# The first modulations of a two-block transformer kernel: four column-tiled products on TensorE in place of VectorE sums

## The chip, the cores and the metric

One core of a Trainium2 chip. The metric is the device time of one execution in microseconds (us); the kernel before is given as the median of three runs. TensorE (PE) does matrix products, with its weight loads shown apart as PEld; VectorE (DVE) and ScalarE (ACT) do the elementwise work; SyncE (SP) issues nearly all loads from memory, in the order of its queue.

## The reference, cut to what matters

Two transformer blocks run one after the other over 256 tokens of 1024 numbers, all in f32. The first block begins with a modulation: a vector `c` (for the tokens) and a vector `c_ctx` (for 256 context tokens) each go through silu and are multiplied by the matrix `w_ada`, 1024 rows by 6144 columns. Only the first 2048 columns, the shift and the scale ahead of attention, are touched here:

```
mod_x = silu(c) @ w_ada + b_ada        # sh1 = columns 0..1023, sc1 = columns 1024..2047, ...
mod_c = silu(c_ctx) @ w_ada + b_ada
h  = rms_norm(x, g_attn) * (1 + sc1) + sh1
hc = rms_norm(ctx, g_attn) * (1 + csc1) + csh1
```

`h` and `hc` then go through the q, k and v projections, attention, a mixture of 32 experts (12 MB of weights each), and a second block with its own modulations.

## The kernel before

Everything named here is in `attention_block`. An order of the instructions on each engine is worked out by a planner when the program is built, from its own estimate of the times; each engine then keeps that order and waits where an input is late. An instruction later in the program text can be put ahead of an earlier one that is not expected to be ready. `high_priority` raises the rank of what stands under it, and the modulation steps for later use (`ada_step`) run at a lowered rank (LOW1).

Start. SP loads x and ctx (L317, L319) and then, through the stream `g.w1`, the eight 1 MB tiles that hold the 2048 columns. They go into a pool of four buffers (NSTAGE), so that tile 4 can be loaded only when one of the first four has been used up. The same pool and the same queue serve the projections' weights (`in_w_qkv`), which come right behind. `cs` is silu of the two vectors, 128 partitions by 2 by 8. PE normalizes and transposes x and ctx (L349) and transposes x once more (L354); ACT copies the results out (L350, L355).

Modulations. ADA1 gives the order in which the eight tiles come: four of them hold 1024 shift columns for 256 rows, the other four 512 scale columns for 512 rows. `shifts` multiplies a tile by the vector's numbers, one partition at a time, and adds it to `acc`, on DVE (L368, L370), sixteen operations on 128x1024. `scales` does the rest as products on PE with two stationary columns (L379), copies the rows out on ACT (L383) and turns them into columns (L386). At the end sixteen products with ones (L394) sum `acc` over the partitions. The results stand in `pt`; DVE makes `mod` of them in three small operations (L397, L399, L400).

What `mod` starts. ACT makes `hh` (L418, sixteen operations), DVE the rest `hl` (L420, L422), and PE the first projection from them (L593). The projection's weights are split beforehand in halves of a tile: ACT makes `hi` (L141), DVE `lo` (L142); three halves are made ahead of the first use. DVE also sums the later modulations from half-tiles of `w_ada` and `ada_w` (L190, L192), one operation for each 0.5 MB load, with two buffers of their own.

The experts' products further on (L918) show one form that matters here: `products` sends two products with 64 stationary columns each to the two halves of one bank of PSUM,

```
on = o[n] if e == WIDE else o[0][n * SLOTS:(n + 1) * SLOTS]
g.got = pe.matmul(out=on, lhsT=x, rhs=w[:, n * 512:n * 512 + 512], start=first, stop=last)
```

Of the kernel before, what the change touches and what calls it, by code (L numbers as in the profile page):

```python
# [8 lines left out]
F32 = mybir.dt.float32  # L9
# [4 lines left out]
ALU = mybir.AluOpType  # L14
# [7 lines left out]
NL0 = 8  # L22
ADA_PLACES = 30
LOW1 = 200

ADA1 = (0, 1, 0, 1, 0, 0, 1, 1)
ADA1_SUM = 7
ADA_RET = 12
ADA_F0 = 12
ADA_D0 = 4  # L30
# [25 lines left out]
def bc(ap, dim, n):  # L56

    a = list(ap.ap)
    a.insert(dim, [0, n])
    return bass.AP(tensor=ap.tensor, offset=ap.offset, ap=a)  # L60
# [89 lines left out]
def rsqrt(nc, pool, ss, n, scale, tag, e=None):  # L150

    v, e = nc.vector, e or nc.vector
    x = ss if scale is None else pool.tile([128, n], F32, tag=tag + "x", name="rsx")
    y, h, t = (pool.tile([128, n], F32, tag=tag + k, name="rs" + k) for k in "yht")
    if scale is not None:
        v.tensor_scalar(out=x, in0=ss, scalar1=scale, scalar2=EPS, op0=ALU.mult, op1=ALU.add)
    v.tensor_scalar(out=y.bitcast(I32), in0=x.bitcast(I32), scalar1=-0.5, scalar2=float(0x5F3759DF), op0=ALU.mult, op1=ALU.add)
    e.tensor_scalar(out=h, in0=x, scalar1=-0.5, scalar2=None, op0=ALU.mult)
    for _ in range(3):
        if n <= 2:  # L160
            cols = [slice(i, i + 1) for i in range(n)]
            for i in cols:
                e.tensor_scalar(out=t[:, i], in0=y[:, i], scalar1=y[:, i], scalar2=h[:, i], op0=ALU.mult, op1=ALU.mult)
            for i in cols:
                e.tensor_scalar(out=y[:, i], in0=t[:, i], scalar1=1.5, scalar2=y[:, i], op0=ALU.add, op1=ALU.mult)
        else:
            v.tensor_tensor(out=t, in0=y, in1=y, op=ALU.mult)
            v.tensor_tensor(out=t, in0=t, in1=h, op=ALU.mult)
            v.scalar_tensor_tensor(out=y, in0=t, scalar=1.5, in1=y, op0=ALU.add, op1=ALU.mult)
    return y  # L170
# [123 lines left out]
def attention_block(tc, g):  # L294

    nc, A, ws = tc.nc, g.A, g.ws
    v, s, pe = nc.vector, nc.scalar, nc.tensor
    xT1 = g.xT1
    with ExitStack() as es:
# [6 lines left out]
        def bank(name="b"):  # L306
            return ps.tile([128, 512], F32, tag="b", name=name)

        def bank1(tag):
            return pss.tile([128, 512], F32, tag=tag, name=tag)  # L310
# [3 lines left out]
        pl = es_x.enter_context(tc.tile_pool(name="pl", bufs=1))  # L314
# [13 lines left out]
        cs = c1.tile([128, 2, 8], F32, name="cs")  # L328
# [26 lines left out]
            s.copy(out=xT1[:, k:k + 2], in_=b.rearrange("p (k t) -> p k t", k=2))  # L355


        pt = bank("pt")
        acc = [pl.tile([128, 1024], F32, name=f"acc{j}") for j in range(2)]

        def shifts(i):
            w = g.w1.get()
            for k in range(2):
                wk = w[:, k * 1024:(k + 1) * 1024]
                for j in range(2):
                    cc = cs[:, j, 2 * i + k:2 * i + k + 1]
                    if i == k == 0:
                        v.tensor_scalar(out=acc[j], in0=wk, scalar1=cc, scalar2=None, op0=ALU.mult)  # L368
                    else:
                        v.scalar_tensor_tensor(out=acc[j], in0=wk, scalar=cc, in1=acc[j], op0=ALU.mult, op1=ALU.add)  # L370

        def scales(i):
            w = g.w1.get()
            b4, h = divmod(i, 2)
            if h == 0:
                pms.append(bank("pm"))
            pm = pms[-1]
            for k in range(4):
                pe.matmul(out=pm[:2, :], lhsT=cs[:, :, h * 4 + k], rhs=w[:, k * 512:(k + 1) * 512],  # L379
                          start=(h == 0 and k == 0), stop=(h == 1 and k == 3))  # L380
            if h == 1:
                row = pl.tile([2, 512], F32, tag="row", name="row")
                s.copy(out=row, in_=pm[:2, :])  # L383
                for j in range(4):
                    m = 8 + b4 * 4 + j
                    pe.transpose(out=pt[:, 2 * m:2 * m + 2], in_=row[:, j * 128:(j + 1) * 128], identity=g.ident[:2, :2])  # L386

        pms = []
        for i, kind in enumerate(ADA1):
            (scales if kind else shifts)(sum(k == kind for k in ADA1[:i]))  # L390
            if i == ADA1_SUM:
                for j in range(2):
                    for m in range(8):
                        pe.matmul(out=pt[:, 2 * m + j:2 * m + j + 1], lhsT=acc[j][:, m * 128:(m + 1) * 128], rhs=g.ones[:, :1], start=True, stop=True)  # L394
        mod = c1.tile([128, 16, 2], F32, name="mod")
        with tc.high_priority():
            v.tensor_tensor(out=mod, in0=pt[:, :32].rearrange("p (m j) -> p m j", j=2),  # L397
                            in1=bc(g.pv("b_ada")[:, :16], 2, 2), op=ALU.add)
            v.tensor_scalar(out=mod[:, 8:], in0=mod[:, 8:], scalar1=1.0, scalar2=None, op0=ALU.add)  # L399
            v.tensor_tensor(out=mod[:, 8:], in0=mod[:, 8:], in1=bc(g.pv("g_attn"), 2, 2), op=ALU.mult)  # L400

# [13 lines left out]
        for k in range(8):  # L415
            for j in range(2):
# [4 lines left out]
                                scalar2=mod[:, k, j:j + 1], op0=ALU.mult, op1=ALU.add)  # L421
# [181 lines left out]
        for t in range(4):  # L603
# [7 lines left out]
            else:  # L611
                v.tensor_tensor(out=ko[:, kt].rearrange("p (n d) -> p n d", d=64), in0=kq.rearrange("p (n d) -> p n d", d=64),
                                in1=bc(gn[:, 2], 1, 2), op=ALU.mult)
        r = rsqrt(nc, sm, sk, 8, 1.0 / 64, "k")
        v.tensor_tensor(out=ko.rearrange("p t (n d) -> p (t n) d", d=64), in0=ko.rearrange("p t (n d) -> p (t n) d", d=64),
                        in1=bc(r, 2, 64), op=ALU.mult)
# [11 lines left out]
        r = rsqrt(nc, sm, sq, 16, 1.0 / 64, "q")  # L628
        for t in range(2):
            q2 = tp.tile([128, 512], F32, tag="qq", name="qq")  # L630
            v.tensor_tensor(out=q2.rearrange("p (c j d) -> p j c d", j=2, d=64),
                            in0=qo[t].rearrange("p (j c d) -> p j c d", j=2, d=64),
                            in1=bc(r[:, 8 * t:8 * t + 8], 2, 64).rearrange("p (j c) d -> p j c d", j=2), op=ALU.mult)
# [17 lines left out]
        for t in range(2):  # L651
# [8 lines left out]
            for m in range(2):  # L660
                r = slice(64 * m, 64 * m + 64)
# [16 lines left out]
        shifts = o1.tile([128, 1024], F32, name="shifts")  # L678
# [11 lines left out]
        acc = bank1("t")  # L690
# [1207 lines left out]
def tile_body(ctx, tc, A, out):  # L1898
# [85 lines left out]
    g.s5dram = [nc.dram_tensor(f"s5_scratch_{c}", (128, S5W), F32, kind="Internal").ap() for c in range(8)]  # L1984
    g.s5E = [nc.dram_tensor(f"s5_scratch_e{c}", (128, 2, 16, 64), F32, kind="Internal").ap() for c in range(2)]
    attention_block(tc, g)
    g.ws.stream.load(19, es_hx.enter_context(tc.tile_pool(name="hx", bufs=1, side="right")).tile([128, 2048], F32, name="hx"))
    g.angp = ctx.enter_context(tc.tile_pool(name="angp", bufs=1))
# [13 lines left out]
def host_arrays(inputs):  # L2002
    import numpy as np

    def cat(*a):
        return np.ascontiguousarray(np.concatenate(a, axis=0))

    def colblocks(w, nb, kper):

        K, N = w.shape  # L2010
        t = w.reshape(K // (128 * kper), kper, 128, N // nb, nb).transpose(3, 0, 2, 1, 4)
        return t.reshape(-1, 128, kper * nb)
# [5 lines left out]
    d = {}  # L2018
    d["x"], d["ctx"] = I["x"][0], I["ctx"][0]
    wa = I["w_ada"][0]  # L2020
    ada1 = cat(colblocks(wa[:, :1024], 1024, 2), colblocks(wa[:, 1024:2048], 512, 4))
    d["w_ada1"] = ada1[np.argsort(np.argsort(ADA1, kind="stable"))]
    d["w_ada2"] = colblocks(wa[:, 2048:], 1024, 2)
    wq = I["w_qkv"][0]
    d["w_qkv"] = cat(colblocks(wq[:, 512:768], 256, 8), colblocks(wq[:, :512], 512, 4),
# [26 lines left out]
    cs = [I[f"s5_{n}_2"][0].reshape(8, 4, 2, 16, 64).transpose(0, 2, 4, 1, 3).reshape(8, 128, 4, 16) for n in ("c_re", "c_im")]  # L2052
# [20 lines left out]
    f = np.float32  # L2073
# [5 lines left out]
    row = np.broadcast_to(np.arange(4, dtype=f)[:, None], (4, 64)).reshape(-1)  # L2079
# [3 lines left out]
    c, s = np.cos(ang).astype(f), np.sin(ang).astype(f)  # L2083
# [28 lines left out]
```

## Time and profile before

| | |
|---|---|
| median of 3 runs | 2090.07 us (2088.04 to 2090.89) |
| the profiled execution | 2090.91 us |
| its span, first to last instruction | 2089.2 us |
| TensorE clock, mean over the span | 0.977 of full speed |
| busy: PE, DVE, ACT | 93%, 54%, 31% of the span |
| read from memory | 626.79 MB, 307 GB/s over the span |

The profile is of one execution. The busy share of PE counts time in which a product is under way, and does not mean that PE works at its peak. All times in the rows count from the first instruction of the span. In a row of the timeline the first two numbers are start and duration, then come the engine, the line, the operation and the tiles (written <- read), the shape and the count; in brackets is the idle time of the engine ahead of it and what ended that.

### The profile page before, as it was taken

Reading aid. Unit: us, or ns where it says so; the run is one execution under the profiler, and the core shown is the slowest. Engines: PE = TensorE matmul, PEld = TensorE weight load, DVE = VectorE, ACT = ScalarE, POOL = GpSimd, SP = SyncE. Lnnn points to the kernel's source line nnn. Section 1 sums busy time; section 2 is a strip of 40 time slices with the busy share of each in tenths; the row PEclk is TensorE's granted clock in tenths of the full one; section 3 lists DMA queues with packets and bytes.
Section 4 is the critical chain, followed back from the end, with each engine's and each line's share of the span. In section 5 each row is a group of like instructions: output and inputs, shape, how many; then the busy total and the mean of one; then the engine's idle time right before and its main releaser. Section 6 shows DMA issues by size and latency. Waiting matters only on the chain. (4 is left out here: it accounts for less than half of the span.)

```text
span 2089.2 us, 29010 instructions
## 1 busy us (share of the span) xinstructions
PE 1951.1 (93%) x11166; PEld 1246.5 (60%) x11166; DVE 1125.1 (54%) x2378; ACT 648.0 (31%) x1135; POOL 59.2 (3%) x92
## 2 busy tenths in 40 slices
PE   6999989999999989999998997999999999899998
PEld 3856844444333333332333326888999999599998
DVE  5865765132222212221222127999898978768863
ACT  3464311000000000000000004446677645256542
POOL 0000000000000000000000000000001002100000
PEclk9999989999999999999999998999999999799999
DMA  8656559999999999999999994667857778655651
GB/s 315 223 162 221 207 224 365 405 379 375 421 421 421 421 421 420 422 421 421 421 421 421 421 414 160 228 221 273 301 213 249 271 286 296 211 186 192 223 182 61
DMA packets 101757, 643.40 MB, mean 308 GB/s; under 512 B 11584, under 2 KB 12880, under 8 KB 34288
## 3 DMA queue, kind: packets, MB, share of 16 engines
q1 hardware_dynamic: 94176, 613.46, 75.1%
q0 software_dynamic: 6624, 26.76, 3.8%
q8 instruction: 89, 1.46, 0.3%
q10 hardware_dynamic: 816, 1.30, 0.2%
q14 instruction: 52, 0.43, 0.1%
HBM read 626.79 MB, written 14.68 MB: 307 GB/s over the span
## 5 line engine op out<-in xcount | busy, mean ns | idle before, releaser
L918 PE MATMUL hc<-w,xe 128*64 128x512 f32 (+1 forms) x2008 | 476.1, 598 | 54.1 <-DMA w<-in_w_in_dram 54.0
L918 PEld LDWEIGHTS hc<-w,xe 128*64 128x64 f32 (+1 forms) x2008 | 142.4, 138 | 375.3 <-issue 218.4
L142 DVE TENSOR_TENSOR lo<-w,hi 128x1024 fp32r<-128x1024 f32 x238 | 289.1, 1219 | 75.0 <-ACT hi L141 74.0
L141 ACT CAST hi<-w 128x1024 fp32r<-128x1024 f32 x238 | 249.0, 1049 | 253.0 <-PE b L241 156.7
L240 PE MATMUL b<-h2h,hi 128*128 128x256 f32 x896 | 254.6, 285 | 10.7 <-ACT h2h L1729 9.1
L938 DVE COPY hs<-hc 128x512 f32<-128x512 f32 x33 | 22.8, 691 | 448.8 <-PE hc L918 448.8
L241 PE MATMUL b<-h2l,hi 128*128 128x256 f32 x896 | 254.5, 285 | 0.2
L242 PE MATMUL b<-h2h,lo 128*128 128x256 f32 x896 | 253.9, 284 | 0.0
L918 PE MATMUL yb<-w,hb 128*64 128x512 f32 (+1 forms) x1024 | 252.6, 604 | 0.5 <-DMA w<-in_w_out_dram 0.5
L240 PEld LDWEIGHTS b<-h2h,hi 128*128 128x128 f32 x896 | 169.8, 190 | 13.3 <-ACT h2h L1729 9.3
L241 PEld LDWEIGHTS b<-h2l,hi 128*128 128x128 f32 x896 | 169.7, 190 | 4.0 <-issue 1.1
L242 PEld LDWEIGHTS b<-h2h,lo 128*128 128x128 f32 x896 | 169.7, 190 | 0.4 <-issue 0.4
L936 ACT COPY hs<-hc 128x512 f32<-128x512 f32 x33 | 19.3, 585 | 464.2 <-PE hc L918 464.2
L918 PEld LDWEIGHTS yb<-w,hb 128*64 128x64 f32 (+1 forms) x1024 | 66.8, 137 | 127.5 <-issue 119.5
L192 DVE SCALAR_TENSOR_TENSOR acc<-w,c,acc 128x1024 f32<-128x1024 f32 x77 | 98.4, 1278 | 12.0 <-DMA w<-in_ada_w_dram 11.4
L240 PE MATMUL b<-ah,hi 128*128 128x256 f32 x352 | 100.3, 286 | 0.0
L242 PE MATMUL b<-ah,lo 128*128 128x256 f32 x352 | 99.9, 284 | 0.2 <-DVE lo L142 0.2
L241 PE MATMUL b<-al,hi 128*128 128x256 f32 x352 | 99.4, 283 | 0.0
L981 ACT COPY ys<-yb 64x512 f32<-64x512 f32 (+1 forms) x32 | 18.5, 578 | 243.1 <-PE yb L918 243.1
L900 PEld LDWEIGHTS gb<-S,h 128*128 128x128 f32 x544 | 66.7, 197 | 37.2 <-issue 25.8
L1009 DVE TENSOR_TENSOR yacc<-sc,yacc 128x512 f32<-128x512 f32 x68 | 46.7, 688 | 66.5 <-PE sc L1007 66.5
L900 PE MATMUL gb<-S,h 128*128 128x128 f32 (+1 forms) x544 | 74.9, 289 | 1.2 <-DVE S L891 1.2
(523 smaller groups left out, 3061.1 us busy)
## 6 DMA issues: line engine op xcount, KB each, us to landing
w<-in_w_in_dram SPq DMA_DIRECT2D x252, 1024.0 KB, 13.1
w<-in_w_out_dram SPq DMA_DIRECT2D x128, 1024.0 KB, 14.5
w<-in_ffn_up_dram SPq DMA_DIRECT2D x44, 1024.0 KB, 5.0
w<-in_ada_w_dram SPq DMA_DIRECT2D x72, 512.0 KB, 5.0
w<-in_ret_w_in_dram SPq DMA_DIRECT2D x24, 1024.0 KB, 5.1
w<-in_ffn_down_dram SPq DMA_DIRECT2D x22, 1024.0 KB, 5.1
w<-in_w_ada_dram SPq DMA_DIRECT2D x32, 512.0 KB, 4.5
w<-in_ada_w_dram POOLq DMA_DIRECT2D x24, 512.0 KB, 4.8
```

Of the source, the lines that this page charges most:

```text
L141: self.nc.scalar.copy(out=hi, in_=w)
L142: self.nc.vector.tensor_tensor(out=lo, in0=w, in1=hi.bitcast(F32), op=ALU.subtract)
L192: v.scalar_tensor_tensor(out=self.acc, in0=w, scalar=cc, in1=self.acc, op0=ALU.mult, op1=ALU.add)
L240: pe.matmul(out=o, lhsT=w[0][:, sl], rhs=a[0][:, k], start=first, stop=False)
L241: pe.matmul(out=o, lhsT=w[0][:, sl], rhs=a[1][:, k], start=False, stop=False)
L242: pe.matmul(out=o, lhsT=w[1][:, sl], rhs=a[0][:, k], start=False, stop=last)
L900: g.got = pe.matmul(out=b[:, k * 128:k * 128 + n], lhsT=g.h2[:, t, d * 128:(d + 1) * 128], rhs=S[:, t, :n], start=(t == 0), stop=(t == 1))
L918: g.got = pe.matmul(out=on, lhsT=x, rhs=w[:, n * 512:n * 512 + 512], start=first, stop=last)
L936: s.copy(out=h, in_=hc[e][n])
L938: v.tensor_copy(out=h, in_=hc[e][n])
L981: s.copy(out=o, in_=i)
L1009: v.tensor_tensor(out=y, in0=b, in1=y, op=ALU.add)
```

## The change

All 2048 columns go through PE. The eight tiles are now blocks of 128 rows by 2048 columns. `cz` holds the two numbers of each row, padded with zeros to 32 stationary columns. For each tile k four products with 512 moving columns each go to the four groups of 32 partitions of one bank `pm`, and add up over k. One ACT copy brings the bank to SBUF, four whole 128x128 transposes turn it, and DVE picks out the two columns of each group of 32. `acc`, the DVE operations on it, the sixteen products with ones and the order ADA1 are gone; copy and transposes stand under `high_priority` now.

```
-        def shifts(i): ...
-        def scales(i): ...
+        cz = pl.tile([128, 8, 32], F32, name="cz")
+        v.memset(cz, 0.0)
+        v.tensor_copy(out=cz[:, :, :2], in_=cs.rearrange("p j k -> p k j"))
+        pm = bank("pm")
+        for k in range(8):
             w = g.w1.get()
...
+            for c in range(4):
+                pe.matmul(out=pm[32 * c:32 * c + 32, :], lhsT=cz[:, k], rhs=w[:, c * 512:(c + 1) * 512], start=(k == 0), stop=(k == 7))
         mod = c1.tile([128, 16, 2], F32, name="mod")
         with tc.high_priority():
-            v.tensor_tensor(out=mod, in0=pt[:, :32].rearrange("p (m j) -> p m j", j=2),
-                            in1=bc(g.pv("b_ada")[:, :16], 2, 2), op=ALU.add)
+            row = pl.tile([128, 512], F32, name="row")
+            s.copy(out=row, in_=pm)
+            pt = bank("pt")
+            for m in range(4):
+                pe.transpose(out=pt[:, m * 128:(m + 1) * 128], in_=row[:, m * 128:(m + 1) * 128], identity=g.ident)
+            v.tensor_tensor(out=mod.rearrange("p (c m) j -> p c m j", c=4), in0=pt.rearrange("p (m c r) -> p c m r", m=4, c=4)[:, :, :, :2],
+                            in1=bc(g.pv("b_ada")[:, :16].rearrange("p (c m) -> p c m", c=4), 3, 2), op=ALU.add)
...
-    ada1 = cat(colblocks(wa[:, :1024], 1024, 2), colblocks(wa[:, 1024:2048], 512, 4))
-    d["w_ada1"] = ada1[np.argsort(np.argsort(ADA1, kind="stable"))]
+    d["w_ada1"] = colblocks(wa[:, :2048], 2048, 1)
```

## Rows read from the trace of the kernel before

**Rows 1.** The page, busy time of each engine over the whole span.

```profile
PE 1951.1 (93%) x11166; PEld 1246.5 (60%) x11166; DVE 1125.1 (54%) x2378; ACT 648.0 (31%) x1135; POOL 59.2 (3%) x92
```

**Rows 2.** Timeline from 16 us to the first modulation products on PE.

```profile
16.52 1.22 PE L349 MATMUL b<-dg,xr 128*128 128x128 f32 x4 [16.52 <-DVE dg L345]
16.96 1.41 DVE L368 TENSOR_SCALAR acc<-w,cs 128x1024 f32<-128x1024 f32 x2
...
22.01 9.65 DVE L370 SCALAR_TENSOR_TENSOR acc<-w,cs,acc 128x1024 f32<-128x1024 f32 x8
...
25.17 1.91 PE L354 MATMUL b<-ident,xr 128*128 128x128 f32 x16
...
27.01 7.03 PE L379 MATMUL pm<-w,cs 128*2 128x512 f32 x16
```

**Rows 3.** Timeline from there to the start of the first projection.

```profile
31.86 4.87 DVE L370 SCALAR_TENSOR_TENSOR acc<-w,cs,acc 128x1024 f32<-128x1024 f32 x4 [0.20 <-DMA w<-in_w_ada_dram]
...
35.60 7.03 PE L379 MATMUL pm<-w,cs 128*2 128x512 f32 x16 [0.49 <-DMA w<-in_w_ada_dram]
...
36.65 0.75 DVE L190 TENSOR_SCALAR acc<-w,cs 128x1024 f32<-128x1024 f32 x1
...
41.72 1.04 ACT L141 CAST hi<-w 128x1024 fp32r<-128x1024 f32 x1 [7.07 <-DMA w<-in_w_qkv_dram]
42.72 0.57 ACT L383 COPY row<-pm 2x512 f32<-2x512 f32 x1
...
43.69 4.17 PE L394 MATMUL pt<-ones,acc 128*128 128x1 f32 x32
47.90 0.19 DVE L397 TENSOR_TENSOR mod<-pt,pvt 128x32 f32<-128x32 f32 x1 [3.88 <-PE pt L394]
...
48.21 1.22 DVE L142 TENSOR_TENSOR lo<-w,hi 128x1024 fp32r<-128x1024 f32 x1
49.34 0.17 DVE L400 TENSOR_TENSOR mod<-mod,pvt 128x16 f32<-128x16 f32 x1
...
49.55 7.99 ACT L418 ACTIVATE hh<-xT,mod 128x256 fp32r<-128x256 f32 x16 [4.29 <-DVE mod L400]
...
50.20 0.58 PE L593 MATMUL b<-hi,hh 128*128 128x256 f32 x1 [2.34 <-ACT hh L418]
```

**Rows 4.** Instructions on tile pm to 60 us: duration minimum/median/maximum, ns.

```profile
L379 PE MATMUL pm<-w,cs x32: 589/592/592, 27.0 to 42.0; 128*2 128x512 f32 x32
```

**Rows 5.** Timeline of the two experts' products of 64 columns, at 600 us.

```profile
599.96 1.94 PE L918 MATMUL hc<-w,xe 128*64 128x512 f32 x8 [0.55 <-DMA w<-in_w_in_dram]
```

**Rows 6.** SP's issues of loads, single ones out of narrow windows.

```profile
26.90 0.33 SPq L109 DMA_DIRECT2D w<-in_w_ada_dram  x1
30.64 0.33 SPq L109 DMA_DIRECT2D w<-in_w_ada_dram  x1
...
49.83 0.43 SPq L109 DMA_DIRECT2D w<-in_w_ada_dram  x1
```

**Rows 7.** Loads into the tiles w to 50 us, issue to landing.

```profile
DMA to landing us min/median/max: 4.8/7.2/14.5
```

**Rows 8.** Windows: length; busy PE, PEld, DVE, ACT, POOL; clock; DMA; GB/s.

```profile
36.00:38.00 2.00, 2.00 (x6) 0.42 (x5) 1.40 (x2) 0.00 (x0) 0.00 (x0) 1.00 1.02 422
46.00:48.00 2.00, 1.86 (x13) 1.77 (x12) 0.10 (x1) 0.00 (x0) 0.00 (x0) 0.70 0.68 287
70.00:80.00 10.00, 10.00 (x44) 8.04 (x43) 10.00 (x24) 4.87 (x8) 0.00 (x0) 1.00 0.86 306
```

**Rows 9.** Timeline of DVE and ACT, first projection, from start to end.

```profile
50.56 1.05 DVE L420 TENSOR_SCALAR xT<-xT,mod 128x256 f32<-128x256 f32 x3
...
59.96 1.21 DVE L142 TENSOR_TENSOR lo<-w,hi 128x1024 fp32r<-128x1024 f32 x1
61.09 0.68 DVE L422 TENSOR_TENSOR hl<-xT,hh 128x512 fp32r<-128x512 f32 x1
...
62.58 0.27 ACT L606 COPY kq<-b 128x128 f32<-128x128 f32 x1 [3.15 <-PE b L593]
```

**Rows 10.** DVE's sums for later modulations (L192), windows: length, busy, clock, DMA, GB/s.

```profile
40.00:80.00 40.00, 5.10 (x4) 0.91 0.70 255
80.00:120.00 40.00, 11.49 (x9) 0.91 0.62 206
```

More of the change, by code (lines that the diff above doesn't have):

```diff
@@ L24 @@
 LOW1 = 200
-ADA1 = (0, 1, 0, 1, 0, 0, 1, 1)
-ADA1_SUM = 7
 ADA_RET = 12
@@ L355, in attention_block @@
             s.copy(out=xT1[:, k:k + 2], in_=b.rearrange("p (k t) -> p k t", k=2))
-        pt = bank("pt")
-        acc = [pl.tile([128, 1024], F32, name=f"acc{j}") for j in range(2)]
-        def shifts(i):
-            w = g.w1.get()
[L363 to L394, printed above, removed]
+        cz = pl.tile([128, 8, 32], F32, name="cz")
+        v.memset(cz, 0.0)
+        v.tensor_copy(out=cz[:, :, :2], in_=cs.rearrange("p j k -> p k j"))
```

## The prediction

> **What bounds the kernel now.** I read the page first, then the timeline of the first 62 us on every engine, then SP's issues, then windows over the same stretch. Over the span PE counts as busy for 93% and DVE for 54% [rows 1], but that mean says nothing of the start, where the change sits.
>
> At the start PE is idle until 16.5 us and then holds L349 and L354 until 27.08. The first modulation products begin only there, at 27.01, although their inputs do not depend on L349. DVE meanwhile sums the shift tiles: tile 0 from 16.96, tiles 2 and 4 from 22.01 [rows 2]. So DVE gives buffers back early, PE gives its own back late. The last tile bounds the rest: the second set of PE products starts at 35.60 after a wait for a load, and ends at 42.63. Then comes a tail: copy 0.57, transposes, 4.17 us of products with ones, and `mod`. In that tail DVE waits 3.88 us for the products with ones, and a `lo` of 1.22 us slips between the second and the third operation on `mod`. `hh` begins at 49.55, the projection at 50.20 [rows 3]. That is what the change can shorten.
>
> **The change part by part.**
>
> *DVE.* Sixteen sums go: two in 1.41 us, the others at 9.65/8 = 1.21 us each, 18.3 us in all [rows 2]. They ran from 17 to 37 us. After the last of them DVE had one operation to do ahead of the first `lo` [rows 3]. So they filled idle time, and I count them at nothing by themselves; the filling of the `cz` tile, two small operations in the idle start, too. What idle DVE does instead comes below.
>
> *PE products.* An f32 product shows as two records: 32 records are the 16 products of L379, 0.59 us each [rows 4], and they follow each other at 14.06/16 = 0.88 us a product [rows 2, 3]. The change has 32 products of the same 512 moving columns. End to end they need 28.1 us. Before shows no product with four tiles side by side; the nearest row is the experts' pair of 64-column tiles: 8 records, four products, take 1.94 us, where 4 x 0.88 = 3.5 would stand end to end [rows 5]. Two run at once there. So a loaded tile of weights costs 3.5 us (one at a time), 1.76 (in pairs) or 0.88 (four at once). I take 0.88, since that pair has the form of this change, one stationary operand size per tile and different moving columns; 1.76 and 3.5 stay as bounds. [...]
>
> *The loads.* Now every buffer comes back through PE, and not before 27.0. With 0.88 a tile and 0.16 of tail (0.59 less 0.43), tile 0 is free at 28.1; SP issues tile 4 at once, as before it issued within 0.1 us of the release (30.64 after the fourth product of L379) [rows 3, 6]. In before a tile load went out at 26.90 already [rows 6]. The shortest landing is 4.8 us [rows 7], and at 422 GB/s a 1.05 MB tile follows each 2.5 us [rows 8]. Tiles 4 to 7 land at 32.9, 35.4, 37.9 and 40.4, and the last four products end at 41.4. That is 1.2 us ahead of 42.63. In pairs: tile 4 goes out at 28.9, tile 7 lands at 41.2, end 43.1. The loads set it, so even half the concurrency costs only 1.7 us.
>
> *The projection's weights.* They use the buffers of tiles 4 to 7, so they queue right behind: the first lands at 42.9, the second at 45.4. In before the first cast ran from 41.72 [rows 3]: 1.2 us worse.
>
> *The tail.* Copy 0.58, four transposes at 1.91/16 = 0.12 plus latency, 0.6 [rows 2], three operations on `mod`, 0.55 without a `lo` between them [rows 3]: 1.8 us. Before it was 49.55 - 42.63 = 6.9. Best case, nothing in between: `hh` at 43.3, 6.2 us earlier. Worst case: ACT keeps its planned order. In before one cast stood ahead of the last row copy (41.72 against 42.72) [rows 3]. If the planner expects the products to be slow, all three casts made ahead stand before the copy: the third ends at 45.4 + 1.05 = 46.5, and `hh` starts at 48.4, 1.2 us earlier than before. I take this, since the row of before shows the start of that order.
>
> *What is late next.* DVE. Its L420 to L422 chain runs from 50.56 to 61.77, with one `lo` of 1.21 in it [rows 9]: 10.0 us of its own, and PE's products end with it, when ACT goes on at 62.58. The three `lo` made ahead (3.7 us) must be done on either side of it. With the casts first they are done by then: L420 starts at 48.9, and the chain ends at 60.1, 1.6 us earlier; from PE's start it is about 1.1. With `hh` first the chain starts at 43.8 but has four `lo` in it: 43.8 + 10.0 + 4.9 = 58.7, 3.1 us earlier. So a tail 5 us shorter is worth 1.1 to 3.1 here: the rest goes into DVE work that only moves. I take 1.5.
>
> *Idle DVE.* From 17 to 43 us DVE has next to nothing. Before already pulled one later sum (L190) into such a gap, at 36.65 [rows 3], while the load of its partner was issued only at 49.83 [rows 6]. From 70 to 80 us DVE is full [rows 8], and four such sums, 5.1 us, lie between 40 and 80 [rows 10]. Each sum pulled ahead saves 1.28 us there. Bounds: none, 0; four, 5.1. I take one, 1.3.
>
> *Sum.* 1.5 + 1.3 = 2.8 us at about 85 us. Behind that, no row shows a fixed time to which work would have to wait, so I let it pass to the end. 2090.91 - 2.8 = 2088.1 for the profiled execution, whose span of 2089.2 has 1.7 us around it; the median of the runs is 0.84 below it, so 2087.3. A difference under 0.2% (4.2 us) can hardly be told from no change.
>
> **The rivals.**
>
> *No concurrency (slower).* The products run one at a time at 32 columns. Then PE ends at 27.0 + 28.1 = 55.1, `hh` at 57, all `lo` done: the chain ends some 6.9 us later, 2097. It decides from a group cost above 2.5 us, where PE and not the loads sets the pace. Against it: the pair [rows 5]. Chance 0.08.
>
> *A later sum stands ahead of `mod` on DVE (slower).* Place: DVE's queue between the last old work and `mod`. L190 stood there in before [rows 3]; if its partner L192 does too, and its load goes out at 49.8 as before [rows 6], it lands near 54.6 [rows 7], and `hh` starts near 56.5: 7 us later, 2097. It decides as soon as that load lands after 47. Chance 0.10; other orders that lose, 0.04.
>
> *PE takes the first groups ahead of L349 or within it (faster).* Tile 0 was there by 16.96 [rows 2], so tile 4 could go out near 18 and the loads never pause. Tile 7 then lands near 32, and the chain is some 9 us earlier: 2081. Against it: L379 stood behind all of L354 though tiles 1 and 3 made it wait for nothing [rows 2]. Chance 0.10.
>
> *Four or more sums are pulled ahead (faster).* 1.5 + 5.1 = 6.6 us, 2083.5. For it: DVE is empty for 25 us and the loads pause. Against it: SP issued the second load so late. Chance 0.14; other orders that win, 0.06.
>
> *The clock takes it back (no gain).* Granted clock was 0.70 of full in 46 to 48 us, behind the products with ones [rows 8]. Now PE has 0.9 us of products in each 2.5 us of loads from 31 to 41 and may fall to the lower of its two levels sooner: last group 0.9 more, transposes 0.5, projection started slow for longer, up to 1.5. With the casts first the copy waits anyway, so it costs 0.5 to 2: 2089. [...] No row of before has such a stretch of this kernel. Chance 0.06.
>
> **How the numbers follow.** The forecast has 0.42, with a range of its own of 2085.9 to 2089.7 (gain 0.4 to 4.2: pairs and no sum pulled, up to `hh` first and one sum). Faster: 0.10 + 0.14 + 0.06 = 0.30. Slower: 0.08 + 0.10 + 0.04 = 0.22. Same: 0.42 + 0.06 = 0.48. The range 2081 to 2096.5 reaches to the early loads below and nearly to the two slow cases above.
>
> **What would show it.** Right: no DVE sums before 43 us, groups of eight records near 1 us each, the last four ending near 41, no load of tiles 4 to 7 issued before 28, `hh` between 43 and 48.5, DVE's chain ending near 59 to 60. Wrong: groups of 3.5 us; a load of tile 4 near 18; several L192 before 45 us; DVE waiting for a half-tile load ahead of `mod`; or an earlier projection whose lead is gone by 300 us, where the experts begin.

## The result, and the profile after

The changed kernel is slower. Its median is 2101.2 us (4 runs, 2098.66 to 2102.93), that of the kernel before in the same comparison 2089.06 us (4 runs); the ratio is 1.0055, 95% interval 1.004 to 1.007. The profiled execution took 2099.77 us. A ratio compares undisturbed runs alone, so it need not be the quotient of two medians.

The page, busy time over the span. It answers to [rows 1], and taken alone it would have suggested a gain: PE, DVE and ACT all do a little less.

```profile
PE 1944.8 (93%) x11162; PEld 1241.5 (59%) x11162; DVE 1110.8 (53%) x2364; ACT 647.5 (31%) x1134; POOL 59.2 (3%) x92
```

The timeline from the first pulled sum to the first projection, for [rows 2, 3]. Line numbers are 27 lower behind the change: L418 is L391, L141 is L138, L593 is L566.

```profile
24.10 0.75 DVE L187 TENSOR_SCALAR acc<-w,cs 128x1024 f32<-128x1024 f32 x1 [5.67 <-DMA w<-in_w_ada_dram]
...
28.21 3.64 PE L362 MATMUL pm<-w,cz 128*32 128x512 f32 x32
28.55 1.28 DVE L189 SCALAR_TENSOR_TENSOR acc<-w,cs,acc 128x1024 f32<-128x1024 f32 x1 [1.85 <-DMA w<-in_w_ada_dram]
34.22 1.07 PE L362 MATMUL pm<-w,cz 128*32 128x512 f32 x8 [2.36 <-DMA w<-in_w_ada_dram]
...
41.63 1.94 PE L362 MATMUL pm<-w,cz 128*32 128x512 f32 x8 [0.55 <-DMA w<-in_w_ada_dram]
43.64 0.58 ACT L366 COPY row<-pm 128x512 f32<-128x512 f32 x1 [14.52 <-PE pm L362]
...
44.27 1.11 PE L369 MATMUL pt<-ident,row 128*128 128x128 f32 x4 [0.70 <-ACT row L366]
...
46.13 7.97 ACT L391 ACTIVATE hh<-xT,mod 128x256 fp32r<-128x256 f32 x16 [1.91 <-DVE mod L373]
...
54.01 3.87 ACT L138 CAST hi<-w 128x1024 fp32r<-128x1024 f32 x4
...
55.09 1.22 PE L566 MATMUL b<-hi,hh 128*128 128x256 f32 x4 [9.71 <-ACT hi L138]
...
57.58 0.69 DVE L395 TENSOR_TENSOR hl<-xT,hh 128x512 fp32r<-128x512 f32 x1
57.72 0.58 PE L566 MATMUL b<-lo,hh 128*128 128x256 f32 x1 [1.41 <-DVE lo L139]
```

What was meant to be fast is fast. Eight records, four products with one tile of weights, take 1.07 us: the four column tiles work at once. The last products end at 43.57 and `hh` starts at 46.13, 3.4 us before the 49.55 of [rows 3]. DVE's chain ends at 58.27, 3.5 us before the 61.77 of [rows 9]. But ACT makes all sixteen `hh` before the first cast, and PE waits 9.71 us for that cast: the projection starts at 55.09, where it started at 50.20. Its weights had been issued from 35.3 us on; the first load landed 8.7 us later, near 44.

Windows over the same stretch, columns as in [rows 8]. The granted clock falls from 1.00 to 0.50, the lower of the two levels seen in these traces, between 34 and 36 us (0.87 in that window), while the groups wait for loads, and is back only after 62 (0.80 in 62 to 64). From 36 us on a group takes 1.94 us, and nearly the first 8 us of the projection pass at 0.50. In the kernel before the first 3.4 us of the projection did so too (last row, 0.55 over 4 us).

```profile
34.00:36.00 2.00, 1.07 (x8) 0.16 (x8) 0.00 (x0) 0.00 (x0) 0.00 (x0) 0.87 1.02 430
36.00:46.00 10.00, 6.92 (x28) 1.32 (x28) 0.50 (x3) 0.58 (x1) 0.00 (x0) 0.50 1.01 426
46.00:54.00 8.00, 0.00 (x0) 0.00 (x0) 7.16 (x19) 7.87 (x16) 0.00 (x0) 0.50 0.95 379
54.00:62.00 8.00, 5.50 (x24) 5.21 (x25) 8.00 (x13) 3.88 (x5) 0.00 (x0) 0.50 0.20 52
62.00:64.00 2.00, 2.00 (x16) 2.00 (x16) 1.97 (x2) 0.00 (x0) 0.00 (x0) 0.80 1.03 426
```

```profile
50.00:54.00 4.00, 3.80 (x17) 3.51 (x18) 4.00 (x10) 4.00 (x10) 0.00 (x0) 0.55 0.89 302
```

Behind the projection two more things differ. The first is in DVE's sums for later modulations. Windows of those sums alone (length, busy, clock, DMA, GB/s), the changed kernel:

```profile
80.00:120.00 40.00, 8.95 (x7) 1.00 0.59 206
120.00:145.00 25.00, 0.00 (x0) 1.00 0.02 4
145.00:175.00 30.00, 10.27 (x8) 0.94 0.62 214
```

and the kernel before, which made nine in the first of these stretches [rows 10]:

```profile
120.00:145.00 25.00, 8.96 (x7) 1.00 0.50 165
145.00:175.00 30.00, 7.18 (x6) 1.00 0.43 142
```

No sum and nearly no load for 25 us. The changed kernel's timeline shows what stood there:

```profile
114.63 1.28 DVE L189 SCALAR_TENSOR_TENSOR acc<-w,cs,acc 128x1024 f32<-128x1024 f32 x1
...
139.63 0.28 PE L200 MATMUL s<-ones,acc 128*128 128x1 f32 x2
143.63 1.72 PE L200 MATMUL s<-ones,acc 128*128 128x1 f32 x14
145.39 0.17 DVE L202 TENSOR_TENSOR mod<-s,pvt 128x8 f32<-128x8 f32 x1 [1.49 <-PE s L200]
145.48 0.74 DVE L187 TENSOR_SCALAR acc<-w,cs 128x1024 f32<-128x1024 f32 x1
...
196.32 3.54 PE L200 MATMUL s<-ones,acc 128*128 128x1 f32 x16 [3.49 <-DVE acc L189]
```

Eight sums make a group in one tile `acc`, which exists once. The group is complete at 115.9 us; its products with ones stand in PE's order until 145.35, and only then may the next group begin. Before, the products of that group ran from 124.44 and the next group began at 126.40. The fourth group is late for it: it is full at 196.2 us for 182.1 before, and PE waits 3.49 us for its last sum. (L200 has eight products, sixteen records, a group.) Behind that wait the clock is at 0.50 until 206 us. All engines from 195 to 210 us, columns as in [rows 8], the changed kernel and then the kernel before, where a shorter stretch at half clock began at 190 us (0.54 in 190 to 192, 0.50 to 196, 0.75 in 196 to 198):

```profile
195.00:210.00 15.00, 12.29 (x36) 7.68 (x37) 8.38 (x17) 4.99 (x11) 0.00 (x0) 0.66 0.97 381
```

```profile
195.00:210.00 15.00, 14.32 (x48) 7.38 (x47) 11.44 (x32) 10.29 (x25) 0.00 (x0) 0.93 0.49 190
```

The kernel before has a pause too, from 147.06 to 161.38 us, for the same reason; its fourth group is full in time all the same.

The second is the start of the experts. The first 48 records of the experts' products, the products with `b_out`, and the 39 records behind them, in the timeline of before:

```profile
286.91 10.52 PE L918 MATMUL hc<-w,xe 128*64 128x512 f32 x48
...
303.44 2.93 PE L1029 MATMUL yb<-bout,gT 32*128 32x512 f32 x6
...
315.24 9.17 PE L918 MATMUL hc<-w,xe 128*64 128x512 f32 x39
```

and of the changed kernel:

```profile
296.94 10.52 PE L891 MATMUL hc<-w,xe 128*64 128x512 f32 x48
313.46 3.79 PE L1002 MATMUL yb<-bout,gT 32*128 32x512 f32 x6
...
328.62 9.17 PE L891 MATMUL hc<-w,xe 128*64 128x512 f32 x39
```

The lag is 10.0 us ahead of this place and 13.4 behind it: 328.62 less 315.24. At the end 8.9 of it are left (spans of 2098.1 and 2089.2 us).

### The profile page after: what moved, and what is told of

Read it like the earlier page. It is cut to its first block, busy times and chain, and to the rows that moved or that the text cites. A ratio compares the mean times of both kernels' runs of the same rounds, so it can differ in the third digit from the quotient of the medians.

```text
span 2098.1 us, 28982 instructions
## 1 busy us (share of the span) xinstructions
PE 1944.8 (93%) x11162; PEld 1241.5 (59%) x11162; DVE 1110.8 (53%) x2364; ACT 647.5 (31%) x1134; POOL 59.2 (3%) x92
## 5 line engine op out<-in xcount | busy, mean ns | idle before, releaser
L138 ACT CAST hi<-w 128x1024 fp32r<-128x1024 f32 x238 | 248.9, 1050 | 260.5 <-PE b L238 166.1
```

Of the source, the lines that this page charges most:

```text
L138: self.nc.scalar.copy(out=hi, in_=w)
```

## The experiments

Four theories. A: the order on ACT, all casts behind `hh`, costs the time. B: something holds up the later sums at 116 to 145 us; at first I took SP's queue, where a tile of `w_o` waits, later the place of the products with ones on PE. C: the clock. D: any change of the planner's order moves the time by several us. The texts in quotation below stood before each run.

| version | median us (runs) | ratio to before, 95% interval |
|---|---|---|
| changed kernel | 2101.2 (4) | 1.0055 [1.004, 1.007] |
| the same, with the second set | 2106.02 (6) | 1.0079 [1.0054, 1.0104] |
| casts first | 2088.7 (12) | 0.9999 [0.9984, 1.0013] |
| casts first, and warm | 2087.84 (12) | 1.0000 [0.9984, 1.0015] |
| warm only | 2104.38 (6) | 1.0084 [1.0058, 1.011] |
| before, casts last | 2096.14 (11) | 1.003 [1.0015, 1.0045] |
| before, plan moved | 2095.86 (12) | 1.0033 [1.0014, 1.0051] |
| w_o on POOL's queue | 2097.75 (12) | 1.0032 [1.0016, 1.0049] |
| products with ones at plain rank | 2090.72 (12) | 1.0014 [0.9995, 1.0032] |
| before, the same | 2090.4 (12) | 1.0013 [0.9995, 1.0031] |
| casts first, full rows | 2083.64 (12) | 0.9977 [0.9955, 0.9999] |
| the same again | 2086.66 (12) | 0.998 [0.9961, 0.9998] |
| casts first, warm, full rows | 2085.47 (12) | 0.9981 [0.9965, 0.9997] |
| before, full rows | 2087.54 (12) | 0.9994 [0.9976, 1.0012] |
| changed, full rows | 2099.95 (12) | 1.0048 [1.0028, 1.0069] |
| casts first, full rows, ones at plain rank | 2091.16 (12) | 1.0008 [0.999, 1.0026] |

Before itself had medians of 2087.82 to 2090.66 in the later four comparisons, each on a chip of its own, so versions of different comparisons are set against each other by their ratios.

**Casts first** (A). `Parts.get` is cut in two, and its first half, `fill`, which makes the casts, is called ahead of `hh`:

```
+        ws.fill()
         for k in range(8): ... s.activation(out=hh[:, k, sl], ...)
```

> The changed kernel with one edit: the first three casts of the projection's weights (hi, lo) stand ahead of hh in the program text, so that the planner can put them ahead of or between the hh operations on ScalarE, where the changed kernel has all 16 hh first. Theory A (the late first cast, 54.0 us, holds TensorE's projection to 55.1, and TensorE is the bound from there to 190 us): the projection starts near 47 to 48, and the time falls by about 7, to some 2094. Theory B (the loss is made later, where SP's queue is blocked by a load of w_o from 116 to 144 us): under 3 us, 2098 to 2101. Theory C (TensorE at half clock from 35 to 63 us): the projection starts earlier but at half clock, 2 to 4 us gained, about 2098.

The loss is gone, where A alone had forecast 2094. The timeline of this version:

```profile
44.87 0.60 ACT L396 ACTIVATE hh<-xT,mod 128x256 fp32r<-128x256 f32 x1 [1.91 <-DVE mod L377]
45.38 1.98 ACT L138 CAST hi<-w 128x1024 fp32r<-128x1024 f32 x2
...
46.46 0.80 PE L571 MATMUL b<-hi,hh 128*128 128x256 f32 x2 [2.33 <-ACT hi L138]
```

The projection starts 8.6 us earlier than in the changed kernel; 1.3 us of that is an earlier `mod`. But the pause at 120 to 145 us is gone too (five sums there; one of 22.5 us comes later, from 137.9 to 160.4), so this run alone doesn't tell A from B. The fourth group is full at 182.9 us, nearly as in before, and PE doesn't wait for it. In these traces a pause costs PE a wait only where it makes a group late. And this version is no gain against before, though its first experts' products start at 283.26, 3.65 us ahead of before.

**Before, casts last** (A alone): in the kernel before the same `fill` stands behind the last `hh`.

```
+        with tc.issue_after(last.ins):
+            ws.fill()
```

> The kernel before with the reverse edit: the first casts are tied behind the last of the 16 hh on ScalarE; nothing else. Theory A: hh runs from about 46 to 54 or 49 to 57, the first product of the projection comes 5 to 8 us later than 50.2, and the time rises by 5 to 8, to 2094 to 2097. Theories B and C: no or little loss, within 3 us of 2089, unless the queue or the clock changes too, which its trace would show.

It is slower by 0.15 to 0.45%, with the projection from 57.08 us, 6.9 us late where the changed kernel's was 4.9, and no pause in the sums at 120 to 145 us (seven there). The order on ACT by itself, in the kernel before, costs about half of the loss.

**Before, plan moved** (D): the rank of the later sums, LOW1, is 160 for 200.

> A control: the kernel before with LOW1 = 160 for 200, which alters nothing that is computed and, by the built program, nothing in the order ahead of the middle of attention, but the planner's order from there to the experts. Theory D (any shift of the plan moves the time by as much as this change did, so that no cause at the start is needed): 4 us or more from 2089, to either side. Theories A to C: within 3 us.

Slower by 0.14 to 0.51%, though in its profiled execution the experts start within 0.4 us of before (287.23 for 286.91); that execution took 2091.62 us, less than the median, and doesn't show where the rest is lost. So D holds in part: a difference of some 5 us between two versions can come from the plan alone, and is put down below to an edit only where the profile shows its place.

**Casts first, and warm; warm only** (C). Four more products per tile, whose result nothing reads, keep PE busy between loads; in the second version without the edit to the casts.

```
+                pe.matmul(out=pz[32 * c:32 * c + 32, :], lhsT=cz[:, k], rhs=xT[:, k], start=True, stop=True)
```

> e1_casts_first with four more column-tiled products for each tile of weights, on other operands and into a bank that nothing reads, to fill TensorE's waits for the loads. Theory C: the granted clock stays at its upper level through 31 to 43 us and the projection is not slowed; 3 us or more below e1_casts_first. Theory A alone: at most 1 us below e1_casts_first, since the projection is then held by VectorE's hl and the casts.

> The changed kernel with four more products per tile of weights, whose result nothing reads, so that PE is busier while it waits for the loads; the order on ACT stays, with all casts behind the sixteen hh. Theory C (the clock): it stays up beyond 35 us, transposes and the first products come sooner, and 2 to 4 us come back. Theory A: PE still waits for the first cast near 53.5 us with nothing to do, the clock falls in that wait, the lag at 60 to 85 us stays within 1.5 us of that of the changed kernel, and the time is 2098 to 2101.

With the casts first the extra products bring the experts' first products to 280.39 us for 283.26, but the time is 0.9 us below "casts first" where C had forecast 3 or more: nothing clear of the intervals. Windows of "warm only":

```profile
34.00:42.00 8.00, 7.67 (x76) 2.25 (x68) 0.00 (x0) 0.00 (x0) 0.00 (x0) 1.00 1.01 426
42.00:44.00 2.00, 1.23 (x12) 0.42 (x4) 0.03 (x1) 0.58 (x1) 0.00 (x0) 1.00 0.98 414
44.00:55.00 11.00, 1.22 (x4) 0.93 (x4) 10.09 (x27) 10.32 (x19) 0.00 (x0) 0.58 0.85 347
```

The clock stays up through the loads (1.00 to 44 us) and falls in the wait for the casts (0.58 in 44 to 55); the projection starts at 53.64 for 55.09 (54.17 in the changed kernel on the same chip), and the time stays that of the changed kernel. C is worth 0.5 to 1.5 us at this place and nothing that the end shows.

**The changed kernel once more, and w_o on POOL's queue** (B, first form). Only the four loads of `w_o` leave SP's queue.

```
+    st.away = range(9, 13)
```

> The changed kernel as it is, for a comparison on the same chip as the runs beside it. Every theory expects what was measured first: some 10 to 12 us above before, 2100 to 2102, if the two sides of the gap belong to the kernels and not to the chip of that measurement. A gap under 6 us would say that the chip or the execution has a share in it.

> The changed kernel; only the four tiles of w_o are loaded on POOL's queue, so that a tile that waits for a buffer no longer holds up the loads for the later sums that stand behind it on SP's queue from 116 to 144 us. The orders of all engines are those of the changed kernel up to 120 us. Theory A (order of casts on ACT): the projection still starts near 55 us, the lag of 7 us at 55 to 85 us stays, and the time is 2099 to 2102. Theory B (SP's queue held up): the lag at 200 us goes from some +9 to +5 us or less, the sums' product that waited 3.5 us at 196 us waits no more, and 3 to 5 us of the loss of 12 come back: 2096 to 2098. If B were the whole cause, 2090.

The lag came out larger on this chip (2106.02), and `w_o` aside gave 8 of its 16 us back: 2097.75, inside the 2096 to 2098 that theory B had forecast, and PE's wait for the fourth group went from 3.94 to 0.44 us. But not by the mechanism named: the sums pause there as well, from 113.7 to 140.1 us, and the lag at 200 us was still 7 where 5 or less was forecast. The windows of the sums in that version:

```profile
120.00:145.00 25.00, 1.60 (x2) 1.00 0.10 27
145.00:175.00 30.00, 8.65 (x7) 0.89 0.49 161
```

The first sum behind the pause, at 140.11 us, again follows the products with ones (138.15 to 139.99). SP's queue was not what held them; that form of B falls. Where the 8 us come from is not shown beyond that shorter wait; the pause ends 5 us sooner (140.1 for 145.1).

**Products with ones at plain rank** (B, second form). They are taken out of the lowered rank of the later sums, in the changed kernel and in before:

```
+                c = todo.pop(0)
                 with tc.high_priority(offset=-LOW1):
-                    todo.pop(0).step((lambda: bank1("s")) if todo else None)
+                    c.step()
+                if todo and c.n % 4 == 0:
+                    c.finish(bank1("s"))
```

> The changed kernel; only the products with ones that end each group of eight later sums (and what DVE does with them) stand at the plain rank and no longer at the lowered one, so that they come as soon as the group is summed. In the changed kernel the second group is summed at 115.9 us, its products with ones end at 145.3, and the tile of sums, which there is once, keeps the next group waiting until 145.5; no load goes out in between. Casts and hh stay as they are. Theory B in its new form (the place of those products in PE's order, not the tile of w_o on SP's queue): the sums go on between 116 and 145 us, the wait of 3.5 us at 196 us goes, and 4 to 8 us of the 12 come back: 2094 to 2098. Theory B in its old form (SP's queue): the sums still pause, since a w_o tile still waits there, and the time stays at 2100 or more. Theory A: the projection starts near 55 us all the same, and it stays slower than before by 4 us or more.

> The kernel before, with nothing but the products with ones at the plain rank. There the sums never stop for 25 us (seven between 120 and 145), so by the new form of theory B it is worth nothing here: within 3 us of before. If it gains or loses more than 4 us, the same edit in the changed kernel moves other things than the pause, and its gain there can't be put down to the pause alone.

This speaks for B in its second form. The changed kernel with that edit, the sums first, then all engines from 195 to 210 us, then the projection and the experts:

```profile
120.00:145.00 25.00, 8.12 (x7) 1.00 0.62 206
```

```profile
195.00:210.00 15.00, 13.48 (x46) 6.48 (x45) 13.24 (x33) 9.86 (x23) 0.00 (x0) 1.00 0.80 317
```

```profile
55.32 1.22 PE L569 MATMUL b<-hi,hh 128*128 128x256 f32 x4 [9.71 <-ACT hi L138]
...
286.27 10.52 PE L894 MATMUL hc<-w,xe 128*64 128x512 f32 x48
...
317.94 9.17 PE L894 MATMUL hc<-w,xe 128*64 128x512 f32 x39
```

The projection is as late as without the edit, 55.32 us, and yet the experts' first products start 0.64 us ahead of the kernel before; the time is 1.0014 of before for 1.0055 to 1.0079 without the edit, some 9 to 14 us less. The wait of 3.49 us at 196 us is gone, and the clock stays at 1.00 behind it. In the kernel before the edit alone brings nothing (1.0013). So most of the loss goes with this edit, which takes out the pause. That the pause alone made that loss is not shown: the edit moves the whole order of the sums. The gain doesn't add up with the loss of "before, casts last", which has no pause at 120 to 145 us and is slower by 3 to 9 us: in the version here the sums not only flow, they run ahead (the group that starts at 161.38 us in before starts at 142.12), and make up for part of the late projection.

**Full rows** (where the lead of "casts first" goes). Its PE led by 3.65 us at the first experts' products and by 0.25 at the 39 records (314.99 for 315.24). In between stand the products with `b_out`, which have 32 rows (from 299.79 to 302.71, and again at 305.41), and the clock falls while PE is busy all the time; windows of "casts first":

```profile
300.00:302.00 2.00, 2.00 (x5) 0.74 (x5) 0.96 (x3) 1.04 (x2) 0.00 (x0) 1.00 1.02 430
302.00:304.00 2.00, 2.00 (x7) 0.83 (x6) 0.38 (x1) 1.99 (x4) 0.00 (x0) 0.72 1.00 422
304.00:306.00 2.00, 2.00 (x3) 0.50 (x2) 1.83 (x4) 0.43 (x1) 0.00 (x0) 0.50 0.19 78
```

The edit fills `bout` and `gT` up with zeros to 128 rows, on top of "casts first":

```
-        bout = bk.tile([32, 1024], F32, name="bout")
+        bout = bk.tile([128, 1024], F32, name="bout")
+        nc.gpsimd.memset(bout, 0.0)
-        gT = bk.tile([32, 256], F32, name="gT")
+        gT = bk.tile([128, 256], F32, name="gT")
+        nc.gpsimd.memset(gT, 0.0)
...
```

> The version with the casts ahead of hh, and one change at 300 us, where the experts begin: the four products with b_out, which have 32 rows, are filled up with zeros to 128 rows. In the version with the casts first PE led by 3.8 us at 300 us and by 0.3 at 315, with the clock at half for 10 us between; in the kernel before it was at half for 3.4 us. If those products of few rows bring the clock down, the stretch at half clock goes or gets shorter, the lead is kept into the experts, and the time is 2084 to 2086. If it is something else (the waits for the experts' first weights, the way that earlier loads fall), the half clock of 10 us stays and the time is 2088 to 2090.

The same place with full rows, windows and timeline:

```profile
300.00:304.00 4.00, 4.00 (x15) 1.45 (x16) 2.32 (x4) 3.18 (x5) 0.00 (x0) 1.00 0.66 279
304.00:308.00 4.00, 4.00 (x22) 1.38 (x20) 0.19 (x1) 0.15 (x1) 0.00 (x0) 1.00 0.02 4
```

```profile
281.53 10.52 PE L896 MATMUL hc<-w,xe 128*64 128x512 f32 x48
...
298.11 2.93 PE L1009 MATMUL yb<-bout,gT 128*128 128x512 f32 x6
...
308.24 9.17 PE L896 MATMUL hc<-w,xe 128*64 128x512 f32 x39
```

The clock stays up, and the lead grows from 5.4 to 7.0 us (281.53 for 286.91, 308.24 for 315.24) where it had gone. Then the edit in the other versions:

> The kernel before, with nothing but the four products with b_out filled up with zeros from 32 to 128 rows. In the kernel before the clock was at half for 3.4 us behind them; products and transposes in that stretch took about 1.6 us more than they take at full clock. If those products bring the clock down, that goes, PE leads by 1.5 to 2 us from 310 us on, and the time is 1 to 3 us below before. If the whole gain of the version with both edits (6.5 us) came from this one, it would be 6 us below before, and the modulations on PE would be worth nothing by themselves.

> The changed kernel with the same filling up alone, the casts still behind the sixteen hh. The lag at 280 us stays at 10 to 12 us, the half clock of 10 us near 315 us goes, and 4 us come back against the changed kernel: 7 to 9 us above before. If the order on ACT is the main cause, it stays slower than before by more than 5 us.

> The version with the casts ahead of hh and the products with b_out filled up, once more, beside the kernel before with the filling up alone, on one chip. If the modulations on PE, with the casts ahead, are worth the lead of 3.8 to 5 us that PE has from 100 to 280 us, this is 3 to 5 us below the kernel before with full rows; if they are worth the 2.8 us of the prediction, 2 to 3; if nothing, the two are equal.

> All three: the casts ahead of hh, four more products per tile to keep PE busy while it waits for loads, and the products with b_out filled up. The extra products gave 1 to 2.5 us of lead at 75 to 280 us before: the lead at 280 us is 6 us, from 320 us on 7.5 to 8.5, and the time is 7 to 9 us below before, if each of the three is kept to the end; equal to the version without the extra products, if what the clock costs ahead of the projection is made good elsewhere.

The clock stays at 1.00 at this place in each of the four. The versions with the casts first and full rows are faster than before by about 0.2% in three comparisons, with intervals that end just below 1; the one with the extra products is some 4 us faster, where 7 to 9 were forecast. Before with full rows alone is not told from before. On one chip "casts first, full rows" is 0.9 us below before with full rows (2086.66 for 2087.54), less than the 3 to 5 that were to show that the lead is kept: in the two profiled executions the experts' first products start at 284.72 and 285.26 us. What the modulations on PE are worth by themselves lies within the measurement. The changed kernel with full rows stays 0.28 to 0.69% slower.

**Casts first, full rows, ones at plain rank.**

> The casts ahead of hh, the products with b_out filled up, and the products with ones at the plain rank. In the version with the first two the sums do not pause for long (five of them between 120 and 145 us), so that little is left to gain: 2083 to 2087, equal to that version, if the pause was the changed kernel's alone; 3 us and more below it, if the groups' waits cost there too.

No gain: 1.0008 of before for 0.9977 and 0.998 without the last edit, some 6 us more by these ratios, though the intervals touch; equality or a gain was expected. Its place is not settled; D may cover it. The edit that gave 9 to 14 us back in the changed kernel gives nothing here or in before.

## Why the prediction was wrong

**The products, the loads, the tail: right.** One tile costs 1.07 us at a granted clock of 1.00 (0.88 taken), the loads set the pace (the last four groups start 2.47 us apart, from 34.22 to 41.63, where 2.5 was taken from [rows 8]), and the last products end 2.2 us behind the forecast of 41.4: the first began 1.2 us later (28.21 for 27.01), and the half clock took 0.9 (1.94 for 1.07). `hh` fell into the range of 43 to 48.5. Four column tiles take 1.07 us where 3.5 stood for them one after another, about 3.3 times as long.

**ACT's order: the step that failed first.** "If the planner expects the products to be slow, all three casts made ahead stand before the copy [...] I take this" was read off one cast ahead of one copy [rows 3]. The opposite came: sixteen `hh`, then the casts. The other bound, `hh` first, I had priced as a gain of 3.1 us, through DVE's chain alone. PE needs a `hi` for its first product too; with sixteen `hh` of 0.5 us ahead of it the first cast ends 8.9 us after `hh` begins. That term was missing: 55.09 for 50.20, a loss of 4.9 us at the start of the projection. DVE's chain did end 3.5 us earlier, for nothing; that it came near the 58.7 of the bound with `hh` first is luck, since it began 3 us later than there (46.77 for 43.8) and had one `lo` in it and not four.

**One later sum pulled ahead, 1.3 us: wrong in kind.** Three were pulled (from 24.10 to 29.83 us), where before had one; the prediction's own list of signs, which calls no sum before 43 us right, contradicts its forecast of one pulled ahead. But a group has eight sums, one tile and an end on PE: sums ahead of time only help if the products with ones come when the group is full. For the first group they did not: it was full at 77.8 us for 90.2 before, and its products ended at 93.0 in both. For the second they stood 24 us behind, and the gain turned into the pause. "no row shows a fixed time to which work would have to wait" overlooked this: [rows 10] counted the sums, and I didn't look for what ends a group. "Ones at plain rank" gives some 9 to 14 of the 12 to 16 us back; a late projection by itself costs 3 to 9 in the kernel before. The two overlap, and how the loss is split between them stays open to some us. Why the planner put the products that late isn't to be seen in a trace; with the casts first it puts them at 109.53 us.

**The clock: mechanism right, price small.** The rival named the stretch and the cause, the waits for a load at each tile. The clock was 0.50 from 36 us on, with waits of 2.36 us at most; with more products in those waits ("warm only") it was 1.00 up to 44 us. Keeping it up gave 0.5 to 1.5 us at the projection (53.64 for 54.17 and 55.09) and nothing at the end. A second half-clock stretch, behind the wait at 196 us, was in no rival.

**"I let it pass to the end": wrong.** The lead of "casts first" was lost at 300 us to another half clock (0.50 in 304 to 312 us), which no row of the prediction looked at.

## What to carry to other kernels

A step that starts earlier is worth nothing until every input of its first consumer is: price the bound by what each engine must still do ahead of it, and read the order of each queue as an assumption with a price on both sides. A planner's order is part of the change: when work moves, look at which buffers are held once, and what ends their use, well behind the edit. And when a lead vanishes, compare the granted clock at the place before looking for a wait.

## What the runs showed of the hardware

The clock fell while PE counted as busy without a break: in "casts first" it was 1.00, 0.72 and 0.50 in the three windows from 300 to 306 us, with PE busy for 2.00 of 2.00 us in each, at and behind products with 32 rows. With the same products filled up to 128 rows it stayed at 1.00 in five profiled executions of four versions, and the products took as long as before (2.93 us for six records). So a wait of PE, which came ahead of the fall at 34 to 36 us, was not needed here; why 32 rows bring the clock down is not shown.

Two profiled executions of one version, "casts first, full rows", have the experts' first products at 281.53 and 284.72 us: the stretch behind 187 us took 2.8 us more in the second, with the same three waits (0.95, 0.72 and 0.67 us). The granted clock was 0.79 in 186 to 194 us and 1.00 in 194 to 202 in the one, 0.60 and 0.76 in the other. A lead of 3 us ahead of such a place is within what one execution differs from the next.
